# The mLSTM projection of a hybrid decoder as eight Strassen pairs, with y through DRAM

## The chip, the cores and the metric

The kernel runs on one core of a Trainium2 chip. The metric is the device time of one execution in microseconds (us); lower is better. Times of whole runs and the profiled execution are told apart below.

## What is computed

One layer of a decoder with two parallel branches, an mLSTM and a sliding-window attention with grouped queries, on 512 prompt tokens and 8 x 4 sample tokens: 544 columns of tokens in all, at a model width of 2048. The part that matters here is the merge:

```python
y = (jax.nn.sigmoid(g_m) * jnp.einsum('btc,cd->btd', br_m, w_proj_m)
     + jax.nn.sigmoid(g_a) * jnp.einsum('btc,cd->btd', br_a, w_proj_a))
out = jnp.einsum('btc,cd->btd', y, w_out)
return _layernorm(DN_ALPHA * x + out, ln_w, ln_b).astype(x.dtype)
```

`br_m` is the mLSTM branch's gated output and `br_a` the attention's; both are 2048 wide, as are the three weight matrices. Everything is float32.

## The kernel before

**Precision.** TensorE multiplies in its `fp32r` form. To keep float32's precision, each operand is split into a high part and the remainder: ScalarE (ACT) casts the high part, VectorE (DVE) subtracts it (`hilo`, lines 237 to 239, for operands; `split`, lines 194 to 200, for weights). A product is three matmuls: high by high, operand's remainder by weights' high part, operand's high part by weights' remainder.

**Layout.** Activations lie with their features on the 128 partitions: 16 tiles of 128 features, each with 544 token columns. A projection gives its output in 16 blocks `ct` of 128 features.

**The plain projection** (`gemm`, line 217, with `products`, line 202): for one block, two loads of 128 x 1024 weights (512 KB each), their splits, and for each of 16 tiles `k` of the contraction three products in two halves of 272 columns: 96 matmuls. The weights come through the pools `wr` (three raw buffers) and `wp` (two buffers of split weights), the result lies in one of two double banks of PSUM.

**The paired projection** (`paired`, line 643, with `prepare`, `half_product` and `gather`): for the input projection, two blocks of output are computed together by Strassen's scheme in Winograd's form. The contraction is cut in two halves of 8 tiles, the tokens in two halves of 272 columns (`HT`), and the two blocks are the third cut. Seven products of 8 x 3 = 24 matmuls, 168 in all, take the place of 192. The seven operands (`XS`) are quarters of the activations and sums of these; the sums of weights are made while the pairs run, some of them by DMAs of GpSimd that add (`acc`). A pair's two outputs lie in two of the three buffers of the pool `ev` until their `end` has stored them. The order of TensorE's instructions is the program's in this stage (`manual_schedule`); all other instructions are ordered ahead of time by the framework, which goes by the program's order, by priorities and by times that it simulates. Tiles of a pool get its buffers in the program's order.

**The stages around the change**, in order:

1. The 72 pairs of the input projection, with attention and the sample tokens' mLSTM in between. They store the sigmoids of the gates to DRAM (`d_sga`, `d_sgm`).
2. The attention's projection, lines 1415 to 1427: 16 plain blocks. A generator for the prompt's mLSTM is stepped every two `k` (`every=2`), and stores `d_brm`. Each block is multiplied by its gate and stored to `d_t`. When the mLSTM is done, its pools are closed (`esA`), and `branch` (line 1227) begins to load `d_brm` and split it, 16 loads of 272 KB and 16 splits, as the operand of the next stage, in a pool `act3` of eight tiles.
3. The mLSTM branch's projection, lines 1429 to 1438: 16 plain blocks. Each block loads its gate and its `d_t`, multiplies and adds, and splits the result at once into `yh` and `yl`, which stay in SBUF in the pool `act` as the next operand.
4. The output projection, lines 1571 to 1605: 13 plain blocks, three more in another form, and the residual and layer norm. Its pool `d1` (z, lw, lb: the input rows, the norm's weights and biases; z is loaded in four pieces of 1 MB, lw and lb are 1 MB each) is opened when the pools of stage 3 are closed.

SP (SyncE) issues all loads and stores here, one after the other; GpSimd issues the adding DMAs.

Of the kernel before, what the change touches and what calls it, by code (L numbers as in the profile page):

```python
# [15 lines left out]
F32 = mybir.dt.float32  # L16
F32R = mybir.dt.float32r
AF = mybir.ActivationFunctionType
ALU = mybir.AluOpType
# [4 lines left out]
NTS = 4  # L24
NS = NB * NTS
T = SEQ + NS
KT = D // 128
MH = 4
MD = 512
# [50 lines left out]
def _build(tc, nc, i, o, es):  # L80
# [11 lines left out]
    V, A, G, PE = nc.vector, nc.scalar, nc.gpsimd, nc.tensor  # L92

    cst = pool(es, "cst", 1, side="left")
    act = pool(es, "act", 8, side="left")
    wr = pool(es, "wr", 3)
    wp = pool(es, "wp", 2)
    evp = pool(es, "ev", 3)
# [19 lines left out]

    def ev(n=T):
        return evp.tile([128, n], F32, tag="ev", name=nm("ev"))  # L120
# [4 lines left out]
    def two(ap):  # L125
        return ap.rearrange("p (a b) -> p a b", a=2)
# [7 lines left out]
    def spawn(g):  # L134
        live.append(g)
# [81 lines left out]
    def gemm(wv, c0, xh, xl, cols=EVEN, raws=(None, None), every=8, prio=0, before=None):  # L217
        ps = mm()
        for half in range(2):
            if before:  # L220
                before(half)
            raw = raws[half] or load_half(wv, c0, half)
            if prio:
                with tc.high_priority(offset=prio):
                    wh, wl = split(raw)
            else:
                wh, wl = split(raw)
            products(ps, half, wh, wl, xh, xl, cols, every)
        return ps

    def pv(ps, r=ALL):
        return ps[r, :, :272]
# [8 lines left out]
    def act_tiles(p, s):  # L241
        return [p.tile([128, 4, T], F32R, tag="act", name=nm(s)) for _ in range(4)]
# [2 lines left out]
        return lambda k, c, w: tiles[k // 4][:, k % 4, c:c + w]  # L245

    HT = T // 2  # L250

    def quad(p, s):
        return [p.tile([128, 8, HT], F32R, tag="act", name=nm(s + n)) for n in "hl"]
# [389 lines left out]
    def paired(work, first=iter(())):  # L643

        steps = [(w, n) for w in work for n in range(7)]
        ready = 0
        load_a(work[0])
        load_b(work[0])
        for at, (w, n) in enumerate(steps):

            while ready < min(at + 3, len(steps)):
                with tc.high_priority(offset=AHEAD):
                    prepare(*steps[ready])
                ready += 1
# [12 lines left out]
            tick()  # L667
# [559 lines left out]
    def branch(src, p, tmp, ahead=()):  # L1227

        hs, los = act_tiles(p, "bh"), act_tiles(p, "bl")

        def steps():
            for k in range(KT):
                if k < len(ahead):
                    st = ahead[k]
                else:
                    st = tmp(k)
                    nc.sync.dma_start(st[:], src[k])
# [176 lines left out]
    bmh = None  # L1414
    for ct in range(16):
        sg = c5t()
        nc.sync.dma_start(sg[:], d_sga[ct])
        ps = gemm(wa_, ct * 128, bah, bal, every=2)
        V.tensor_tensor(out=two(sg[:]), in0=pv(ps), in1=two(sg[:]), op=ALU.mult)
        nc.sync.dma_start(d_t[ct], sg[:])  # L1420
        if bmh is None and (not live or ct == 15):
            drain()
            esA.close()
            esE = ExitStack()
            act3 = pool(esE, "act3", 8)
            bmh, bml, g_ = branch(d_brm, act3, lambda k: c5t() if k % 2 else ev())
            spawn(g_)
    drain()
    yh_, yl_ = act_tiles(act, "yh"), act_tiles(act, "yl")
    yh, yl = whole(yh_), whole(yl_)  # L1430
    for ct in range(16):
        sg, tt = c5t(), ev()
        nc.sync.dma_start(sg[:], d_sgm[ct])
        nc.sync.dma_start(tt[:], d_t[ct])
        ps = gemm(wm, ct * 128, bmh, bml)
        V.tensor_tensor(out=two(sg[:]), in0=pv(ps), in1=two(sg[:]), op=ALU.mult)
# [167 lines left out]
    finish(1, LAST)  # L1604
    drain()
    esD.close()


# [26 lines left out]
```

## Time and profile before

| what | value |
|---|---|
| three runs, us | 2542.88, 2548.21, 2549.33; median 2548.21 |
| profiled execution | 2543.75 us, its span 2541.9 us, granted TensorE clock 0.994 |
| attention's projection | first matmul of its first block at 1806.68 us of the span |
| mLSTM branch's projection | to 2321.70, where the output projection's first matmul starts |
| DMA moved | 421.89 MB, 166 GB/s over the span |

How to read the rows that follow. In a row by window, the numbers are the window, then for each engine its busy time and the number of its instructions, then the granted share of TensorE's clock, the share of time in which the 16 DMA engines are busy, and GB/s. In a row of a timeline there are the start, the duration, the engine (SPq is SP's queue, which issues DMAs), the line, the operation, what it writes and reads, how many, and in brackets the idle time before it and what ended that. In a row of the chain there are the start, the duration, and what ran. In a row of groups there are the line, the engine and the operation, then busy time and the mean of one in ns, then idle time before it and what ended it. Matmuls overlap, so what one costs in a stream is the distance of their starts, not its own duration.

### The profile page before, as it was taken

How to read it: one execution, taken by the hardware profiler on the slowest of the kernel's cores; microseconds unless marked ns; L12 is line 12 of the kernel's file. 1: busy time of each engine (PE TensorE's matmuls, PEld its weight loads, DVE VectorE, ACT ScalarE, POOL GpSimd, SP SyncE). 2: the span in 40 equal slices, each digit the busy share in tenths (PEclk: the TensorE clock that was granted, in tenths of full speed). 3: DMA queues.
4: the chain of work that ended last, by engine and by line, in shares of the span. 5: the costliest groups of instructions: out<-in, count | busy, mean ns of one | idle time of the engine just before them, and what ended most of it. 6: DMA issues, size and time to landing. Idle time of an engine off the chain costs nothing.

```text
span 2541.9 us, 48994 instructions
## 1 busy us (share of the span) xinstructions
PE 2509.8 (99%) x19995; PEld 2443.5 (96%) x19995; DVE 1709.8 (67%) x2506; ACT 1195.5 (47%) x1945; POOL 377.4 (15%) x434
## 2 busy tenths in 40 slices
PE   8999999999999999999999999999999999999997
PEld 7999999999999999999999999999999999999997
DVE  7867677777777777678787788777765653333236
ACT  4447667667667665443434544544533332222221
POOL 2111121111211211132022133121000000000002
PEclk9999999999999999999999999999999999999999
DMA  6566666666666654477577477477654555446332
GB/s 193 136 166 154 161 148 159 153 150 163 147 157 156 151 149 117 108 213 244 154 225 236 137 234 223 139 234 232 216 177 163 168 175 158 132 132 192 109 94 86
DMA packets 537105, 421.89 MB, mean 166 GB/s; under 512 B 43536, under 2 KB 449344, under 8 KB 536592
## 3 DMA queue, kind: packets, MB, share of 16 engines
q1 hardware_dynamic: 526800, 382.05, 50.8%
q0 software_dynamic: 10080, 36.70, 7.9%
q8 instruction: 157, 2.57, 0.4%
q14 instruction: 68, 0.56, 0.1%
HBM read 297.67 MB, written 86.42 MB: 151 GB/s over the span
## 4 chain that ended last, share of the span: by engine, by line
PE 57%; DVE 1%; issue 0%; POOL 0%; DVEq 0%
PE mm L207 21%; PE bank L610 18%; PE bank L612 9%; PE sm L1298 2%; PE sm L1101 1%; PE sm L1330 1%; PE sm L1343 1%; PE sm L207 1%; PE sm L1114 1%; DVE z L1537 0%; PE sm L1277 0%; PE sm L1285 0%; PE sm L1353 0%; DVE z L1542 0%; PE sm L1480 0%
## 5 line engine op out<-in xcount | busy, mean ns | idle before, releaser
L198 ACT CAST wh<-raw 128x1024 fp32r<-128x1024 f32 x604 | 632.3, 1048 | 918.9 <-PE bank L610 505.5
L199 DVE TENSOR_TENSOR wl<-raw,wh 128x1024 fp32r<-128x1024 f32 x604 | 756.5, 1254 | 360.5 <-ACT wh L198 353.1
L610 PE MATMUL bank<-xk,wh 128*128 128x272 f32 x2304 | 318.3, 291 | 0.0
L610 PEld LDWEIGHTS bank<-xk,wh 128*128 128x128 f32 x2304 | 299.5, 189 | 10.0 <-ACT wh L198 7.5
L590 DVE TENSOR_TENSOR raw<-raw,raw 128x1024 f32<-128x1024 f32 x218 | 278.4, 1278 | 6.3 <-DMA raw<-in_w_in 3.4
L207 PE MATMUL mm<-bh,wl 128*128 128x272 f32 x1024 | 214.4, 289 | 0.0
L207 PE MATMUL mm<-bh,wh 128*128 128x272 f32 x1024 | 214.2, 290 | 0.0
L207 PE MATMUL mm<-bl,wh 128*128 128x272 f32 x1024 | 213.4, 288 | 0.0
L612 PE MATMUL bank<-xk,wl 128*128 128x272 f32 x1152 | 167.5, 288 | 0.0
L629 POOL TENSOR_TENSOR ev<-p,ev 128x272 f32<-128x272 f32 x72 | 102.3, 1421 | 428.8 <-ACT ev L628 410.7
L207 PEld LDWEIGHTS mm<-bh,wh 128*128 128x128 f32 x1024 | 160.5, 188 | 2.3 <-issue 2.3
L207 PEld LDWEIGHTS mm<-bl,wh 128*128 128x128 f32 x1024 | 161.8, 188 | 0.0
L207 PEld LDWEIGHTS mm<-bh,wl 128*128 128x128 f32 x1024 | 160.6, 188 | 0.0
L612 PEld LDWEIGHTS bank<-xk,wl 128*128 128x128 f32 x1152 | 154.1, 189 | 0.0
L610 PE MATMUL bank<-n2h,wh 128*128 128x272 f32 x576 | 148.9, 291 | 2.0 <-ACT wh L198 2.0
L610 PE MATMUL bank<-a11h,wh 128*128 128x272 f32 x576 | 149.3, 291 | 0.0
L610 PE MATMUL bank<-s1h,wh 128*128 128x272 f32 x576 | 149.1, 292 | 0.1
L610 PE MATMUL bank<-s4h,wh 128*128 128x272 f32 x576 | 149.0, 292 | 0.0
L610 PE MATMUL bank<-n3h,wh 128*128 128x272 f32 x576 | 148.1, 290 | 0.0
L610 PE MATMUL bank<-a11l,wh 128*128 128x272 f32 x576 | 147.9, 289 | 0.0
L610 PE MATMUL bank<-n2l,wh 128*128 128x272 f32 x576 | 147.3, 288 | 0.0
L610 PE MATMUL bank<-n3l,wh 128*128 128x272 f32 x576 | 146.8, 287 | 0.0
(435 smaller groups left out, 5475.4 us busy)
## 6 DMA issues: line engine op xcount, KB each, us to landing
raw<-in_w_in SPq DMA_DIRECT2D x296, 512.0 KB
raw<-raw POOLq DMA_DIRECT2D x70, 512.0 KB, 4.9
C<-in_state_mlstm_C SPq DMA_DIRECT2D x32, 1024.0 KB
out<-C SPq DMA_DIRECT2D x64, 512.0 KB
raw<-in_w_proj_a SPq DMA_DIRECT2D x32, 512.0 KB
raw<-in_w_proj_m SPq DMA_DIRECT2D x32, 512.0 KB
raw<-in_w_out SPq DMA_DIRECT2D x32, 512.0 KB
d_sgm<-ev SPq DMA_DIRECT2D x16, 272.0 KB
```

The lines of the kernel that those rows point to most:

```text
L198: A.copy(wh[:], raw[:])
L199: V.tensor_tensor(out=wl[:], in0=raw[:], in1=r32(wh[:]), op=ALU.subtract)
L207: PE.matmul(ps[:, f, :w], a[:, kk], b(k, c, w), start=(k == 0 and n == 0), stop=(k == 15 and n == 2))
L590: V.tensor_tensor(out=w[out][:], in0=w[a][:], in1=w[b][:], op=ALU.add)
L610: PE.matmul(ps, wh[:, k], x(p, k), start=(first and k == 0 and p == 0), stop=False, skip_group_check=True)
L612: PE.matmul(ps, wl[:, k], x(0, k), start=False, stop=(k == 7), skip_group_check=True)
L629: G.tensor_tensor(out=c22, in0=p1, in1=c11, op=ALU.subtract)
L1101: PE.matmul(pC[b * 32:b * 32 + 32, :], qz[:, b], ct[:, b], start=True, stop=True, tile_position=(0, b * 32))
L1114: PE.matmul(pus[b][:], Ab[rows, c * 128:c * 128 + 128], r["V4"][rows], start=True, stop=True, tile_position=(b * 32, 0))
L1298: PE.matmul(pp[:, 0:258], a[:, b * 128:b * 128 + 128], b_[:, b, f], start=(b == 0 and n == 0), stop=(b == 3 and n == 2))
L1330: PE.matmul(pp[:, 0:n], x_[c][:, b * 128:b * 128 + 128], y_[c][:, b * 128:SEQ], start=(c == 0 and m == 0), stop=(c == 3 and m == 2))
L1343: PE.matmul(pp[:, 0:258], x_[:, off:off + 128], y_[:, b, f], start=(b == 0 and n == 0), stop=(b == j and n == 2))
```

## The change

The mLSTM branch's projection becomes eight pairs, run by the `paired` of the input projection with adding DMAs.

- Seven operands are needed. Four (`f11`, `f1`, `f2`, `f12`) are built by `first_forms` while the rest of the attention's projection runs, at the place where `branch` stood, in `act3`; two of the sums on the way are stored to DRAM (`d_n3`, `d_s4`). Three (`f3`, `f4`, `f22`) are loaded and split by `last_forms` while the first pair's first products run, in `act`, which the attention's operand leaves. A pool `fr` of four buffers serves these loads.
- Each pair loads its two gates and two tiles of `d_t` into `fr` at its fifth product (`fetch`, called in `paired`), multiplies and adds at its end, and stores y to DRAM (`d_y`). The last pair's two tiles of y stay in SBUF.
- After the pairs, 14 tiles of y are loaded from `d_y` through `ev`, and all 16 are split into `yh` and `yl`, which now lie in `act3`, in the buffers that the first four forms leave. Then `act` and the pairs' pools are closed, and the output projection follows as before, `d1` in the memory that they leave.

```diff
@@ pools and DRAM
-    act = pool(es, "act", 8, side="left")
+    esL = es.enter_context(ExitStack())
+    act = pool(esL, "act", 8, side="left")
...
+    d_y = dr.tile([16, 128, T], F32, name="d_y")
+    d_n3 = dr.tile([8, 128, HT], F32, name="d_n3")
+    d_s4 = dr.tile([8, 128, HT], F32, name="d_s4")
@@ paired
+            if n == 4 and "fetch" in w:
+                w["fetch"]()
@@ behind the mLSTM
+    def branch_part(k, c):
+        st = late["fr"].tile([128, 2, HT], F32, tag="fr", name=nm("fr"))
+        nc.sync.dma_start(st[:], d_brm[k:k + 2, :, c:c + HT].rearrange("k p t -> p k t"))
+        return st[:]
+
+    def first_forms(f11, f1, f2, f12):
+        for k in range(0, 8, 2):
+            ks = slice(k, k + 2)
+            r11, r21, r12, r22 = (branch_part(k_, c) for k_, c in ((k, 0), (k, HT), (k + 8, 0), (k + 8, HT)))
+            hilo(r11, f11[0][:, ks], f11[1][:, ks])
+            yield
+            hilo(r12, f12[0][:, ks], f12[1][:, ks])
+            V.tensor_tensor(out=r22, in0=r22, in1=r21, op=ALU.subtract)
+            yield
+            hilo(r22, f1[0][:, ks], f1[1][:, ks])
+            V.scalar_tensor_tensor(r21, r11, -1.0, r21, op0=ALU.mult, op1=ALU.subtract)
+            nc.sync.dma_start(d_n3[ks].rearrange("k p t -> p k t"), r21)
+            yield
+            V.tensor_tensor(out=r11, in0=r11, in1=r22, op=ALU.subtract)
+            hilo(r11, f2[0][:, ks], f2[1][:, ks])
+            yield
+            V.tensor_tensor(out=r12, in0=r12, in1=r11, op=ALU.subtract)
+            nc.sync.dma_start(d_s4[ks].rearrange("k p t -> p k t"), r12)
+            yield
+
+    def last_forms(f3, f4, f22):
+        for dst, src in ((f3, d_n3), (f4, d_s4), (f22, d_brm[8:16, :, HT:T])):
+            for k in range(0, 8, 2):
+                ks = slice(k, k + 2)
+                st = late["fr"].tile([128, 2, HT], F32, tag="fr", name=nm("fr"))
+                nc.sync.dma_start(st[:], src[ks].rearrange("k p t -> p k t"))
+                with tc.high_priority(offset=AHEAD):
+                    hilo(st[:], dst[0][:, ks], dst[1][:, ks])
+            yield
+
+    def merged(p):
+        w = dict(wv=wm, cA=p * 256, cB=p * 256 + 128, scale=1.0, acc=True)
+        def fetch():
+            w["in"] = []
+            for d_ in (d_sgm, d_t):
+                for ct in (2 * p, 2 * p + 1):
+                    st = late["fr"].tile([128, T], F32, tag="fr", name=nm("fr"))
+                    nc.sync.dma_start(st[:], d_[ct])
+                    w["in"].append(st)
+        def end(o1, o2):
+            g1, g2, t1_, t2_ = w["in"]
+            for ct, o, g, t_ in ((2 * p, o1, g1, t1_), (2 * p + 1, o2, g2, t2_)):
+                V.tensor_tensor(out=g[:], in0=o[:], in1=g[:], op=ALU.mult)
+                V.tensor_tensor(out=g[:], in0=g[:], in1=t_[:], op=ALU.add)
+                if p < 7:
+                    nc.sync.dma_start(d_y[ct], g[:])
+                else:
+                    late[ct] = g
+        w.update(fetch=fetch, end=end)
+        return w
@@ in the attention's projection, when the mLSTM is done
-            act3 = pool(esE, "act3", 8)
-            bmh, bml, g_ = branch(d_brm, act3, lambda k: c5t() if k % 2 else ev())
-            spawn(g_)
+            act3 = pool(esE, "act3", 8)
+            late["fr"] = pool(esR, "fr", 4)
+            wr2 = pool(esR, "wr2b", 3)
+            pe_ = pool(esR, "peb", 1)
+            f11, f1, f2, f12 = (quad(act3, n_) for n_ in ("f11", "f1", "f2", "f12"))
+            spawn(first_forms(f11, f1, f2, f12))
@@ the projection itself
-    yh_, yl_ = act_tiles(act, "yh"), act_tiles(act, "yl")
+    f3, f4, f22 = (quad(act, n_) for n_ in ("f3", "f4", "f22"))
+    XS = [quarter(f) for f in (f11, f1, f2, f12, f3, f4, f22)]
+    with tc.manual_schedule(engines={PE.engine}):
+        open_psum(True)
+        paired([merged(p) for p in range(8)], last_forms(f3, f4, f22))
+    open_psum(False)
+    yh_, yl_ = [], []
+    for q in range(4):
+        for tiles, n_ in ((yh_, "yh"), (yl_, "yl")):
+            tiles.append(act3.tile([128, 4, T], F32R, tag="act", name=nm(n_)))
     yh, yl = whole(yh_), whole(yl_)
     for ct in range(16):
-        sg, tt = c5t(), ev()
-        nc.sync.dma_start(sg[:], d_sgm[ct])
-        nc.sync.dma_start(tt[:], d_t[ct])
-        ps = gemm(wm, ct * 128, bmh, bml)
-        V.tensor_tensor(out=two(sg[:]), in0=pv(ps), in1=two(sg[:]), op=ALU.mult)
-        V.tensor_tensor(out=sg[:], in0=sg[:], in1=tt[:], op=ALU.add)
-        hilo(sg[:], yh_[ct // 4][:, ct % 4], yl_[ct // 4][:, ct % 4])
-    esE.close()
-    esC.close()
+        st = late.get(ct)
+        if st is None:
+            st = ev()
+            nc.sync.dma_start(st[:], d_y[ct])
+        hilo(st[:], yh_[ct // 4][:, ct % 4], yl_[ct // 4][:, ct % 4])
+    esR.close()
+    esL.close()
```

`esE` and `esC` are closed at the end of the kernel instead.

More of the change, by code (lines that the diff above doesn't have):

```diff
@@ L26 @@
 T = SEQ + NS
+HT = T // 2
 KT = D // 128
@@ L245, in whole @@
         return lambda k, c, w: tiles[k // 4][:, k % 4, c:c + w]
-    HT = T // 2
     def quad(p, s):
@@ L1413, in _build @@
     spawn(mlstm())
-    bmh = None
+    esE, esR, late = ExitStack(), ExitStack(), {}
+    def branch_part(k, c):
[21 more added lines that the diff above has]
+            yield
@@ L1420, in _build @@
         nc.sync.dma_start(d_t[ct], sg[:])
-        if bmh is None and (not live or ct == 15):
+        if "fr" not in late and (not live or ct == 15):
             drain()
             esA.close()
-            esE = ExitStack()
             act3 = pool(esE, "act3", 8)
-            bmh, bml, g_ = branch(d_brm, act3, lambda k: c5t() if k % 2 else ev())
-            spawn(g_)
-    drain()
-    yh_, yl_ = act_tiles(act, "yh"), act_tiles(act, "yl")
+            late["fr"] = pool(esR, "fr", 4)
[3 more added lines that the diff above has]
+            spawn(first_forms(f11, f1, f2, f12))
+    drain()
+    f3, f4, f22 = (quad(act, n_) for n_ in ("f3", "f4", "f22"))
[8 more added lines that the diff above has]
+            tiles.append(act3.tile([128, 4, T], F32R, tag="act", name=nm(n_)))
     yh, yl = whole(yh_), whole(yl_)
     for ct in range(16):
-        sg, tt = c5t(), ev()
-        nc.sync.dma_start(sg[:], d_sgm[ct])
-        nc.sync.dma_start(tt[:], d_t[ct])
-        ps = gemm(wm, ct * 128, bmh, bml)
-        V.tensor_tensor(out=two(sg[:]), in0=pv(ps), in1=two(sg[:]), op=ALU.mult)
-        V.tensor_tensor(out=sg[:], in0=sg[:], in1=tt[:], op=ALU.add)
-        hilo(sg[:], yh_[ct // 4][:, ct % 4], yl_[ct // 4][:, ct % 4])
-    esE.close()
-    esC.close()
+        st = late.get(ct)
[5 more added lines that the diff above has]
+    esL.close()
     esD = ExitStack()
@@ L1606, in _build @@
     esD.close()
+    esE.close()
+    esC.close()
 _INS = ["x_prompt", "x_sample", "state_mlstm_C", "state_mlstm_n", "state_mlstm_m", "state_attn_k", "state_attn_v",
```

## The prediction

> **What bounds the kernel now.** I read the page first, then the chain of work that ended last over the projections, then busy time by window, then the timelines of single engines at the two seams that the change makes.
>
> ```profile
> PE 2509.8 (99%) x19995; PEld 2443.5 (96%) x19995; DVE 1709.8 (67%) x2506; ACT 1195.5 (47%) x1945; POOL 377.4 (15%) x434
> ...
> 2099.93 240.00 PE mm L207 x1915
> ...
> 138.00:180.00 42.00, 42.00 (x338) 42.00 (x337) 26.52 (x29) 20.04 (x26) 6.74 (x7) 1.00 0.76 182
> 2060.00:2130.00 70.00, 70.00 (x560) 69.97 (x559) 28.63 (x35) 22.43 (x28) 0.00 (x0) 1.00 0.66 213
> 2130.00:2320.00 190.00, 190.00 (x1519) 190.00 (x1518) 69.36 (x78) 42.52 (x47) 0.00 (x0) 1.00 0.44 130
> ```
>
> TensorE is the bound: in 2130:2320, the mLSTM projection, it has no idle time, while VectorE is busy 69.36 of 190 us and the DMA engines 0.44. The chain is one piece of 1915 matmuls in 240.00 us, 0.1253 us each, across both projections and into the output projection. So every matmul taken out of this stage is worth 0.1253 us, as long as nothing else becomes late.
>
> **The matmuls removed.** Before, 16 blocks of 96 matmuls: 1536 x 0.1253 = 192.5 us. After, 8 pairs of 7 products of 24 matmuls: 1344. A pair bare of other work is in the trace: the window 138:180 holds two pairs, 338 matmuls by the count (2 x 168 and two cut by the window's edges) in 42.00 us, with no idle time. That is 21.0 us each, and 8 x 21.0 = 168.0 us. Term: **-24.5 us**. The counts are fixed by the loops, so the change cannot fail to do this much.
>
> **The pairs' other work.** Each pair's end adds four VectorE operations, and its loads and stores pass DRAM.
>
> ```profile
> L1436 DVE TENSOR_TENSOR c<-mm,c 128x544 f32<-128x544 f32 x15 | 10.9, 725 | 58.8 <-PE mm L207 58.8
> ...
> 89.00:110.00 21.00, 21.00 (x170) 21.00 (x169) 19.75 (x36) 8.87 (x13) 3.04 (x5) 1.00 0.59 145
> 1650.00:1782.00 132.00, 132.00 (x1031) 121.33 (x1030) 104.61 (x120) 58.97 (x76) 26.80 (x39) 1.00 0.75 237
> ```
>
> VectorE: 26.52 / 2 = 13.3 us a pair now, plus 4 x 0.725 = 2.9, so 16.2 of 21; the first pair (89:110) ran at 19.75 of 21.00 and TensorE lost nothing. DMA: that stage already stores two 272 KB tiles a pair; four loads come on top, 1.1 MB in 21 us, 53 GB/s on 182, so 235. The window 1650:1782 moved 237 GB/s with TensorE at 132.00 of 132. SP issues four more loads a pair; the weight loads stand in the same queue behind them, and these have most of a pair's 21 us. GpSimd issues the two adding DMAs a pair as in earlier pairs. Pair 0 also splits f3, f4 and f22: 12 x 0.72 (a split of that size, DVE L239 in the third fence) = 8.6 us of VectorE, which makes about 22 us in the 21 us of that pair with some of it done in the last block before; the cover is the room until products 4, 5 and 6 need them, 12 to 18 us in. If that cover went, it would be a stall of 2 to 3 us once. I take **+1** for the eight pairs (0 to 5).
>
> **The forms built behind the attention's projection.** They replace the old operand's 16 loads and splits by the same number of loads and splits, 16 more VectorE operations (11.6 us) and 8 stores of 272 KB. In 2060:2130 VectorE is busy 28.63 of 70 us, so this fits. Its four steps hang on each other by four buffers: loads, splits and the store behind them make about 12 us a step (two transfers of 4.3 us and some five operations of 0.7, by the rows of the next fence), 50 us from where the old operand was loaded (2072 there) to about 2122. The projection ends at 2321.7 - 192.5 = 2129. Cost 0; the cover is these 7 us, and beyond them each us is a us of waiting ahead of the first pair.
>
> **The seam behind the pairs: y comes back from DRAM.** Before, each block's y is split while the next block runs, and the output projection begins with no gap (row below, 2321.70). After, y of 14 of 16 blocks is loaded again through `ev`, a pool of three buffers, which the pairs use for their two outputs. What a buffer's round costs is in the attention's projection, where the operand is loaded the same way:
>
> ```profile
> 2321.70 0.41 PE L207 MATMUL mm<-yh,wh 128*128 128x256 f32 x2
> ...
> 2072.20 0.76 SPq L1237 DMA_DIRECT2D c<-d_brm  x1
> 2077.96 0.37 SPq L1237 DMA_DIRECT2D c<-d_brm  x1
> ...
> 2076.48 0.65 ACT L238 CAST bh<-c 128x544 fp32r<-128x544 f32 x1 [0.44 <-DMA c<-d_brm]
> ...
> 2077.21 0.72 DVE L239 TENSOR_TENSOR bl<-c,bh 128x544 fp32r<-128x544 f32 x1
> ...
> 1784.02 0.32 SPq L1172 DMA_DIRECT2D d_sga<-ev  x1
> 1787.87 0.32 SPq L1237 DMA_DIRECT2D ev<-d_bra  x1
> ...
> 1809.73 1.70 SPq L1237 DMA_DIRECT2D ev<-d_bra  x2
> ```
>
> Issue at 2072.20, cast begins at 2076.48 (the cast waited for it), split done at 2077.93, next load into that buffer at 2077.96. So 4.28 us to land, 5.8 us a round. The rows of 1784 to 1809 show the same seam once: behind the last pair of the earlier stage one load gets a buffer early (1787.87), the next two only after that pair is over (1809.73), because its two outputs hold the others.
>
> Call E the end of the last pair. The pair before it frees a buffer some 3 us into the last pair, and its first operand's memory, which takes the first y, is free after one product, so from E-18 one buffer works alone: y0 at -18, y1 -12.2, y2 -6.5, y3 -0.7. The last pair's outputs come free when they have been multiplied: some 0.7 us for its last subtraction (an operation of half the size, and its start), 0.725 each for multiply, add, multiply: y4 at 1.5, y5 at 2.9. What happens next decides the case. The memory for z, lw and lb is the one that the pairs' pools and `act` hold, so those loads start when the two y that stay on chip are split: last add done at 3.6, then 0.65 and 0.72 for cast and split, E+5.1 with the gaps. In the kernel before they start at the same sign:
>
> ```profile
> 2324.44 0.72 DVE L239 TENSOR_TENSOR yl<-c,yh 128x544 fp32r<-128x544 f32 x1
> ...
> 2325.02 0.52 SPq L1458 DMA_DIRECT2D z<-in_x_prompt  x1
> ...
> 2336.12 0.38 SPq L191 DMA_DIRECT2D raw<-in_w_out  x1
> 2336.55 5.59 SPq L1466 DMA_DIRECT2D lb<-in_ln_b  x1
> ...
> 2347.32 1.05 ACT L198 CAST wh<-raw 128x1024 fp32r<-128x1024 f32 x1 [6.55 <-DMA raw<-in_w_out]
> ...
> 2325.00:2350.00 25.00, 25.00 (x202) 24.99 (x202) 5.84 (x7) 5.35 (x8) 0.00 (x0) 1.00 1.00 324
> ```
>
> That burst fills all DMA engines for 25 us (share 1.00, 324 GB/s), and a weight load issued within it landed after 11.2 us (2336.12 to 2347.32). Before, nobody needed data then. After, ten loads of y stand in it. By these rows: y6 to y8 are issued at 5.1, 7.3 and 8.7, a round of 11.2 + 1.5 = 12.7, ready at 17.8, 20.0 and 21.4. The third round lies between 5.8 and 12.7 (the burst ebbs); I take 9, nearer to the middle: 26.8, 29.0, 30.4. The last round is quiet: y12 at 32.6, y13 at 34.8. The block's last three steps of six matmuls take 2.25: its end is E+37.0.
>
> TensorE isn't idle all that time, if the order of its queue lets the second block go ahead where the first lacks an operand. At the earlier seam it did:
>
> ```profile
> 1806.60:1829.00 22.40, 18.41 (x137) 17.57 (x137) 1.00 0.63 198
> ...
> 1829.10 0.72 DVE L1419 TENSOR_TENSOR c<-mm,c 128x544 f32<-128x544 f32 x1 [0.27 <-PE mm L207]
> ```
>
> 137 projection matmuls ran before the first block, which has 96, was complete (VectorE takes its result at 1829.10): some 41 are the second block's. Here the second block can go ahead by its first half alone, 48 matmuls, since the two pairs of weight buffers are taken. So 144 matmuls, 18.0 us, are done by E+37.0. Term: **+19.0 us** (y13 ready between 30 and 39: 14 to 23).
>
> **The clock.** The waits come in gaps of one to several us, and a gap costs more than itself:
>
> ```profile
> 118.58 0.39 PE L610 MATMUL bank<-n2h,wh 128*128 128x272 f32 x1 [1.97 <-ACT wh L198]
> ...
> 120.00:124.00 4.00, 4.00 (x24) 4.00 (x23) 1.45 (x2) 1.30 (x3) 0.86 (x1) 0.61 0.69 162
> ```
>
> After an idle time of 1.97 us the granted clock was 0.61 over 120:124, a loss of 0.39 x 4 = 1.6 us. Here most of a slower clock lies within the waiting; what counts is the end of the first block and the return to speed: **+2** (0 to 5). The Trainium skill (TensorE: Matmul & The Clock Gate, Part 1) has the clock halve only after an idle window of about 3.4 us, by which a 2 us gap would be free. The row disagrees; by that rule this term would be 0 as far as the gaps are short.
>
> **The sum** against the profiled execution (2543.75, its span 2541.9): -24.5 + 1 + 0 + 19.0 + 2 = -2.5, so 2541.3. The three runs have a median of 2548.21, 4.5 above the profiled one; on that footing 2545.7, rounded **2546**. About 0.3% (7.6 us) is what a measurement of this kernel tells from no change.
>
> **Rivals.**
> (a) *The burst misses the loads of y* (z's loads put behind them in SP's queue, or later). Every round 5.8: y13 issued at 1.5 + 3 x 5.8 = 18.9, ready 24.7, block done 26.9 to 28.4 with the second block's half; lost about 10, clock 2, pairs 1: -11.5, 2537. For: loads of y come first in the program. Against: at 2325 all of z went out at once as soon as its memory was free. 0.33. The Trainium skill (DMA: Bandwidth & Descriptors, Anatomy of one DMA) gives 2.0 us and the bytes over 436 GB/s for one transfer, 2.64 us for 272 KB as an estimate by that page, and by it this case would come to about 2529; the row says 4.28.
> (b) *Slower: TensorE keeps the blocks' order and stands until y13 is there.* The 48 matmuls don't go ahead (+6.0), and with the burst at full length through the third round (12.7 for 9) y13 is ready at 38.5: +3.7, clock +1: 2546 + 10.7 = 2556.7. It breaks even at y13 about E+31 and shows as slower from E+39. For: the order is fixed beforehand, by simulated landing times. Against: 137 matmuls above. 0.17.
>
> **How the numbers follow.** The forecast, burst and overtaking, has 0.50; its own range is 2539 to 2554. By its bounds it is within 0.3% with 0.80, faster 0.07, slower 0.13. (a) is faster with 0.85, else same; (b) slower with 0.62, else same. Faster 0.035 + 0.28 = 0.32; slower 0.065 + 0.105 = 0.17; same 0.51. The range takes (a) and (b) in: 2535 to 2557.
>
> **What would show it.** Right: eight pairs of 21.0 to 21.2 us from about 2129 to 2298; loads of `d_y` in threes; z's loads between the second and third three; TensorE waiting for `yh` or `yl` with some 20 us in all in the 40 us behind the pairs, the clock under 0.8 there; DMA share near 1. Wrong: pairs longer than 21.6 (VectorE or DMA bound after all); under 10 us of waiting (rival a); z's loads ahead of E or behind the last y; no waiting for y but one at the forms f3 to f22.

## The result, and the profile after

The changed kernel takes 2541.14 us (median of 20 executions, 2536.71 to 2550.3), the kernel before 2548.77 beside it (20 executions): ratio 0.9984, 95% interval 0.9976 to 0.9992. By the ratio that is 4 us or 0.16% faster, within the 0.3% that counts as no change. The two medians are 7.6 us (0.30%) apart, because the executions of one kernel scatter over 10 to 14 us and most of the changed kernel's lie low in their range, most of the other's high; this text goes by the ratio. The profiled execution took 2540.56 us with a span of 2538.8, 3.1 less than before. The forecast of 2541.3 for that execution and "same" held, and the median lies 5 us below its 2546. The sum did not come out as it was written, though: two of its terms were far off, in opposite directions.

The first rows of the page after, its engines; then busy time by window, over the seam ahead of the pairs (2129:2142), over pairs 1 to 7, and behind them:

```profile
PE 2488.7 (98%) x19803; PEld 2420.1 (95%) x19803; DVE 1785.6 (70%) x2606; ACT 1236.5 (49%) x2005; POOL 402.9 (16%) x458
```

```profile
2129.00:2142.00 13.00, 6.58 (x45) 6.38 (x45) 9.31 (x13) 4.82 (x7) 0.00 (x0) 0.82 0.97 244
...
2163.00:2310.00 147.00, 147.00 (x1175) 147.00 (x1175) 102.82 (x120) 59.38 (x72) 21.04 (x20) 1.00 0.89 228
2310.00:2316.00 6.00, 3.37 (x26) 2.96 (x24) 4.96 (x8) 2.89 (x4) 0.00 (x0) 1.00 0.67 204
2316.00:2330.00 14.00, 10.42 (x73) 9.32 (x74) 7.90 (x11) 6.37 (x10) 0.00 (x0) 1.00 0.74 230
```

TensorE has 192 matmuls less and 21.1 us less busy time. In pairs 1 to 7 it never stops: 1175 matmuls in 147.00 us, which is what was forecast. The time is lost on both sides of them: 6.58 busy of 13.00 ahead, 3.37 of 6.00 and 10.42 of 14.00 behind. The chain of waits, which was one piece of 1915 matmuls before, now has DMAs in it at both places:

```profile
2106.12 5.45 DMA fr<-d_brm
2116.84 3.74 DMA d_s<-fr
2120.60 5.87 DMA fr<-d_n
2127.71 2.63 DVE f3l L244 x4
2131.13 6.74 DMA fr<-d_s
2140.07 3.96 PE bank L612 x16
...
2306.90 3.41 DMA ev<-d_y
2314.52 4.20 DMA ev<-d_y
2320.16 2.52 DMA ev<-d_y
2324.14 2.68 DMA ev<-d_y
```

**Ahead of the pairs.** TensorE ends the attention's last block at 2133.65 and starts the first pair at 2140.07. Who it waited for, and the timeline of VectorE, ScalarE and SP's queue:

```profile
PE bank L612 <- DVE c L1484: 6.4, 1, 6.4
```

```profile
2136.25 3.05 DVE L244 TENSOR_TENSOR f4l<-fr,f4h 128x544 fp32r<-128x544 f32 x4 [3.51 <-ACT f4h L243]
2139.21 0.72 DVE L1484 TENSOR_TENSOR c<-mm,c 128x544 f32<-128x544 f32 x1
...
2135.57 0.64 ACT L243 CAST f4h<-fr 128x544 fp32r<-128x544 f32 x1 [7.49 <-DMA fr<-d_s]
...
2128.46 3.21 SPq L1452 DMA_DIRECT2D fr<-d_s  x4
```

Line 1484 multiplies the last block's result with its gate and so clears the PSUM bank. It had its operand at 2133.65 and started at 2139.21, because four splits of the form f4 stood ahead of it in VectorE's queue, and these waited for loads of `d_s4` that were issued from 2128.46, when the four buffers of `fr` came free, and landed in a window with a DMA share of 0.97. VectorE kept to the order that was fixed beforehand: it was idle for 3.51 us ahead of these splits, and for the last 2.6 of these us the block's multiplication, which stood behind them, was ready. The splits themselves then took another 3 us.

**Behind the pairs.** The last product of the last pair ends at E = 2310.55. SP's queue, then VectorE, then TensorE:

```profile
2306.90 0.32 SPq L1511 DMA_DIRECT2D ev<-d_y  x1
...
2309.83 2.26 SPq L1511 DMA_DIRECT2D ev<-d_y  x2
...
2314.52 9.94 SPq L1511 DMA_DIRECT2D ev<-d_y  x7
...
2326.73 0.96 SPq L1511 DMA_DIRECT2D ev<-d_y  x2
2327.73 0.42 SPq L1532 DMA_DIRECT2D z<-in_x_prompt  x1
```

```profile
2311.01 0.73 DVE L244 TENSOR_TENSOR yl<-ev,yh 128x544 fp32r<-128x544 f32 x1 [1.21 <-ACT yh L243]
2311.65 0.72 DVE L1472 TENSOR_TENSOR fr<-fr,fr 128x544 f32<-128x544 f32 x1
2312.29 0.43 DVE L641 SCALAR_TENSOR_TENSOR ev<-bank,p 128x272 f32<-128x272 f32 x1
...
2328.16 1.35 DVE L244 TENSOR_TENSOR yl<-fr,yh 128x544 fp32r<-128x544 f32 x2
```

```profile
PE mm L212 <- ACT yh L243: 2.9, 2, 2.0
PE mm L212 <- DVE ev L641: 2.3, 1, 2.3
PE mm L212 <- DVE yl L244: 0.8, 3, 0.3
```

z's first load is issued right behind the last load of y, at E+17.2. It did not wait for the two y that stay on chip: their splits (`yl<-fr`) start only at 2328.16, and the rest of z follows them from 2329.92. So its place in SP's queue, behind all loads of y, held it back. The burst missed y, and y13's split ended at 2333.35 = E+22.8. TensorE waited 6.2 us in all, 2.3 of them for the last gather (line 641), which again stood behind a split that waited.

### The profile page after: what moved, and what is told of

It reads as the page before. It is cut to its first block, busy times and chain, and to the rows that moved or that the text cites. A ratio compares the mean times of both kernels' runs of the same rounds, so it can differ in the third digit from the quotient of the medians.

```text
span 2538.8 us, 49027 instructions
## 1 busy us (share of the span) xinstructions
PE 2488.7 (98%) x19803; PEld 2420.1 (95%) x19803; DVE 1785.6 (70%) x2606; ACT 1236.5 (49%) x2005; POOL 402.9 (16%) x458
## 4 chain that ended last, share of the span: by engine, by line
PE 54%; DMA 2%; DVE 2%; issue 0%; ACT 0%; POOL 0%; SPq 0%; DVEq 0%; ACTq 0%
PE bank L612 22%; PE mm L212 11%; PE bank L614 11%; PE sm L1302 2%; PE sm L1105 1%; PE sm L1334 1%; PE sm L1347 1%; PE sm L212 1%; DMA raw<-in_w_out 1%; PE sm L1118 1%; DMA ev<-d_y 1%; DVE z L1611 0%; DMA z<-in_x_prompt 0%; PE sm L1281 0%; PE sm L1357 0%
## 5 line engine op out<-in xcount | busy, mean ns | idle before, releaser
L203 ACT CAST wh<-raw 128x1024 fp32r<-128x1024 f32 x628 | 657.3, 1048 | 827.9 <-PE bank L612 595.4
L204 DVE TENSOR_TENSOR wl<-raw,wh 128x1024 fp32r<-128x1024 f32 x628 | 785.6, 1253 | 297.2 <-ACT wh L203 292.8
L592 DVE TENSOR_TENSOR raw<-raw,raw 128x1024 f32<-128x1024 f32 x234 | 298.0, 1275 | 13.1 <-DMA raw<-in_w_proj_m 6.1
L631 POOL TENSOR_TENSOR ev<-p,ev 128x272 f32<-128x272 f32 x80 | 114.4, 1429 | 503.0 <-ACT ev L630 486.9
L590 POOL DMA_DIRECT2D raw<-raw x86 | 74.6, 868 | 458.0 <-DVE raw L592 173.7
L612 PE MATMUL bank<-s4l,wh 128*128 128x272 f32 x576 | 146.7, 287 | 0.0
L612 PE MATMUL bank<-s1l,wh 128*128 128x272 f32 x576 | 146.6, 287 | 0.0
L637 DVE SCALAR_TENSOR_TENSOR ev<-bank,ev 128x272 f32<-128x272 f32 x80 | 35.3, 441 | 120.6 <-PE bank L614 115.5
L612 PEld LDWEIGHTS bank<-n2h,wh 128*128 128x128 f32 x576 | 108.2, 188 | 7.7 <-ACT ev L630 3.4
L612 PEld LDWEIGHTS bank<-s1h,wh 128*128 128x128 f32 x576 | 108.2, 188 | 5.7 <-ACT p L622 2.5
```

The lines of the kernel that those rows point to most:

```text
L203: A.copy(wh[:], raw[:])
L204: V.tensor_tensor(out=wl[:], in0=raw[:], in1=r32(wh[:]), op=ALU.subtract)
L590: G.dma_start(out=w[out][:], in_=w[b][:], accum_op=ALU.add)
L592: V.tensor_tensor(out=w[out][:], in0=w[a][:], in1=w[b][:], op=ALU.add)
L612: PE.matmul(ps, wh[:, k], x(p, k), start=(first and k == 0 and p == 0), stop=False, skip_group_check=True)
L631: G.tensor_tensor(out=c22, in0=p1, in1=c11, op=ALU.subtract)
```

## The experiments

In the single profiles of the changed kernel and the experiments, the attention's last block ended anywhere from 2129.2 to 2139.9 us. Most of that spread comes from stages ahead of the change: the attention's projection began at 1803.5 to 1814.9, and from its first product to its last it took 324.9 to 327.1 us (322.8 before the change). So the experiments are read by the two stretches that the change touches, and by the ratio to the kernel before, run beside each (its median lay between 2543.95 and 2548.77 us). "Head" is from the end of the attention's last block to the start of pair 1; undisturbed it would be 20.9 us (in e8, below). "Seam" is from the last pair's end to the last matmul on y; before the change these matmuls took 206.1.

| kernel | head, us | seam, us | ratio to before, 95% interval |
|---|---|---|---|
| before | | 206.1 | 1 |
| changed | 29.4 | 213.6 | 0.9984 (0.9976 to 0.9992) |
| e1_bank | 26.7 | 214.4 | 0.9966 (0.9953 to 0.9979) |
| e2_forms_behind | 22.0 | 213.5 | 0.9947 (0.9928 to 0.9966) |
| e3_forms_and_sum_behind | 22.1 | 216.5 | 0.9961 (0.9945 to 0.9978) |
| e4_kept_y_first | 28.3 | 236.1 | 1.0047 (1.0027 to 1.0066) |
| e5_five_buffers | 29.6 | 212.4 | 0.9969 (0.9957 to 0.9981) |
| e6_no_overtaking | 29.8 | 215.1 | 0.9978 (0.9968 to 0.9989) |
| e7_no_y_loads | 29.5 | 211.4 | 0.9984 (0.9971 to 0.9997) |
| e8_forms_behind_five_bank | 20.9 | 210.7 | 0.9933 (0.9915 to 0.9951) |
| e9_block_order | 30.1 | 220.0 | 1.0023 (1.0013 to 1.0032) |
| e10_two_y_loads | 30.0 | 205.9 | 0.9960 (0.9945 to 0.9975) |
| e11_splits_behind_gather | 29.7 | 213.5 | 0.9992 (0.9981 to 1.0002) |
| e12_five_edits | 20.9 | 213.0 | 0.9956 (0.9941 to 0.9971) |

How far the stretches scatter can be read from kernels whose edits leave them alone: the head is 28.3 to 30.1 us in the changed kernel, e4 to e7 and e9 to e11, the seam 213.5 to 216.5 in the changed kernel, e2, e3 and e6. Each is one profile, so smaller differences show nothing by themselves.

The theory after the result was: the head is lost to VectorE's queue (f4's splits ahead of the last block's result), the seam to y's loads, one buffer after the other, with z's burst out of the way. Rivals: the head is lost to the change of PSUM pools (the pairs' banks open only when all of the block's banks are clear); the seam is lost to something else than y.

**e1, the banks.** The PSUM pools wait for the single tile whose memory they take, not for the whole pool:

```diff
         if space is None:
             kw["side"] = side or "right"
+        if space in (None, PSUM):
             kw["reuse_waits"] = "tile"
```

> The PSUM pools give back single banks instead of waiting for the whole pool, so the first pair's first product needs no bank of the last attention block. Queue theory (VectorE stands in its queue at f4's splits, which wait for a load, and everything behind them is late): the 6.4 us in front of the first product goes, but the second product then waits for its weights, whose split stands behind the same f4 splits; the first seven products together end at most 3 us sooner, time 0 to 3 us below the changed kernel. Bank theory (the wait is the swap of the PSUM pools): the 6.4 us go and nothing takes their place, 6 to 8 us below.

TensorE's waits in the stretch:

```profile
PE bank L613 <- DVE c L1485: 3.4, 1, 3.4
PE bank L613 <- ACT wh L204: 0.2, 1, 0.2
```

The first product no longer waits, but a later one of the same pair does, for the same operation (now line 1485): the head is 2.8 us shorter of 8.5 lost. The time by the ratios is lower too, but the intervals of the two kernels overlap. The bank decides where the wait is met and a third of its price, not that it is there.

**e2, the forms behind.** The splits of f4 and f22 are tied behind the split of the third weights on ScalarE and VectorE:

```diff
+    if dst is f3:
+        behind = state["wh"].ins, state["wl"].ins
-    with tc.high_priority(offset=AHEAD):
+    with tc.high_priority(offset=AHEAD), ExitStack() as q_:
+        if dst is not f3:
+            [q_.enter_context(tc.issue_after(b_)) for b_ in behind]
         hilo(st[:], dst[0][:, ks], dst[1][:, ks])
```

> The splits of f4 and f22 are ordered behind the splits of the first pair's third weights on VectorE and ScalarE; banks as in the changed kernel. Queue theory: the last attention block's multiplication runs at once, the first pair starts within 1.5 us of the block's end instead of 6.4 and takes 21 to 22 us instead of 23: 6 to 9 us below the changed kernel. Bank theory: the wait in front of the first pair stays above 5 us and the time is within 1 us of the changed kernel.

VectorE, and TensorE's waits in the stretch:

```profile
2132.27 0.72 DVE L1488 TENSOR_TENSOR c<-mm,c 128x544 f32<-128x544 f32 x1 [0.96 <-PE mm L212]
...
2137.69 2.63 DVE L244 TENSOR_TENSOR f4l<-fr,f4h 128x544 fp32r<-128x544 f32 x4
```

```profile
PE bank L612 <- ACT wh L203: 0.9, 1, 0.9
```

The block's result (now line 1488) is taken as soon as TensorE delivers it, f4 follows 5.4 us later and nobody waits for it: the head is 7.4 us shorter, the time 0.37% lower by the ratios, and the intervals of the two kernels are apart. So the queue was the cause, and the cover for the forms was real, only unused.

**e3, the sum as well.** In the last block and the one before it TensorE also lost 1.97 and 0.84 us, its weights' splits standing behind the sum of the first pair's weights and behind a form's subtraction, which waited for loads. Here the sum (line 592) is tied behind the first pair's first split, on top of e2:

```diff
         if n == 1:
             w["t1"] = raw2()
-            add("t1", "b11", "b12")
+            with tc.issue_after(state["wl"].ins) if "fetch" in w else ExitStack():
+                add("t1", "b11", "b12")
```

> As the run before, and the first sum of two raw weights of the first pair is ordered behind the split of its first weights, so that the last attention block's second weights don't wait behind it. Queue theory: the gap of 1.97 us in the last attention block goes too, with 1 to 2 us of clock: 8 to 12 us below the changed kernel. Rival (these gaps cover each other: what is not lost in the block is lost in front of the first pair): the same time as the run before within 1 us.

The gap at the sum went, but the one before it grew from 0.84 to 1.87 us, a weights' split behind a subtraction that had waited 3.38 us for its load:

```profile
2118.39 0.73 DVE L1434 TENSOR_TENSOR fr<-fr,fr 128x544 f32<-128x544 f32 x1 [3.38 <-DMA fr<-d_brm]
2119.03 1.22 DVE L204 TENSOR_TENSOR wl<-raw,wh 128x1024 fp32r<-128x1024 f32 x1
```

No gain over e2 is shown, and the intervals overlap: a miss. The head is the same; the seam is 3 us longer than in e2 behind a wait of 5.4 us for the last gather (2.3 in e2), which the edit doesn't touch.

**e4, the burst.** The two y that stay on chip are split first in the program, so that z's loads come early, as the forecast had assumed:

```diff
-    for ct in range(16):
+    for ct in (14, 15, *range(14)):
         st = late.get(ct)
```

> The two tiles of y that stay on chip are split first, so the buffers under z, lw and lb come free early and their 6 MB of loads start among the loads of y, as the forecast had it. Burst theory of the forecast: loads of y issued within it land after 8 to 12 us instead of 4 to 5, and what is lost behind the pairs is 17 to 23 us instead of 8: 9 to 15 us above the changed kernel. Rival (loads of 272 KB pass between the large ones): at most 3 us above.

SP's queue, the cast of the y that the marked load brings, and TensorE's waits:

```profile
2317.37 0.38 SPq L1532 DMA_DIRECT2D z<-in_x_prompt  x1
...
2330.31 0.38 SPq L1511 DMA_DIRECT2D ev<-d_y  x1
...
2342.70 0.65 ACT L243 CAST yh<-ev 128x544 fp32r<-128x544 f32 x1 [12.17 <-DMA ev<-d_y]
```

```profile
PE mm L212 <- ACT yh L243: 19.8, 5, 11.3
```

z is loaded from E+2.7, a load of y issued at 2330.31 is cast 12.4 us later, and the seam is 22.5 us longer than in the changed kernel. The forecast's mechanism exists, at the forecast's price or more: the seam is 30.0 us above the 206.1 of before, where the forecast had 19.0 and 2 for the clock. By the ratios the kernel is 16 us slower than the changed one, just above the 9 to 15 expected; its executions lie between 2555 and 2568 us, and the profiled one is among the slow ones. Only the condition did not hold in the changed kernel.

**e5, five buffers for y.**

```diff
-            st = ev()
+            st = c5t() if ct % 2 else ev()
             nc.sync.dma_start(st[:], d_y[ct])
```

> Every other load of y takes one of two further buffers, so five instead of three loads of y can be under way. Theory that the seam's 8.2 us are y's loads waiting for buffers (issued one or two at a time from 2295.46 to 2326.73, the next one only when a split has freed a buffer): y13's split is done about 14 us after the last pair's last product instead of 22.9, the waits inside w_out's first two blocks of columns fall from 6.2 us to 2.3 to 3, and the kernel is 3 to 5 us below the changed one, 2536 to 2538. Rival, that the loads are held by the DMA share (0.74 in those 14 us) or that the casts and splits hold y: no more than 1 us below the changed kernel, with the loads issued earlier and landing as much later.

The last split of y ends 17.6 us after the last pair, not 22.8, and the waits for y are gone. Another takes their place:

```profile
PE mm L212 <- DVE ev L641: 3.9, 1, 3.9
PE mm L212 <- ACT wh L203: 0.9, 1, 0.9
```

The waits sum to 5.0 us where they were 6.2, and the seam is 1.2 us shorter. By time it lies below the changed kernel (2538.68; 0.9969 against 0.9984), but the intervals overlap slightly. Between theory and rival: the buffers were a limit for y, and of the 3.7 us of waiting for y that went, 2.5 came back at the gather, which now stood behind a weights' split that had waited 2.65 us for its cast, and at the first weights. The clock took some more: it was 0.50 in 2318.65:2321.15, where the changed kernel's seam had 1.00 throughout. A gain in time is not shown.

**e6, no overtaking.** The edit wraps `gemm` for w_out's first two blocks in a region where TensorE keeps the program's order:

```diff
-        ps = gemm(wo, ct * 128, yh, yl, cols=CUT, raws=raws)
+        with tc.manual_schedule(engines={PE.engine}) if ct < 2 else ExitStack():
+            ps = gemm(wo, ct * 128, yh, yl, cols=CUT, raws=raws)
```

> w_out's first two blocks of columns are put out in the program's order, so that TensorE cannot take the second block's products while the first one's next y is late. Theory that the overtaking hides y's lateness: each of the 48 products of the second block that ran early was cover, 48 x 0.1253 = 6.0 us, so the seam's waits rise from 6.2 to 11 to 13 us and the kernel is 5 to 7 us above the changed one, 2546 to 2548. Rival, that the sum of the waits is set elsewhere (y is early enough for the order not to matter): within 1 us of the changed kernel.

It did not bind: TensorE's instructions stood in the same order as in the changed kernel. So this run says nothing of overtaking and is only a second look at the changed kernel, of use for the clock (last section).

**e7, no loads of y.**

```diff
-            st = ev()
-            nc.sync.dma_start(st[:], d_y[ct])
+            st = late[14 + ct % 2]
```

> This kernel leaves out the 14 loads of y from DRAM: all 16 y tiles are splits of the last pair's two kept tiles (so w_out gets a wrong operand by design of the experiment); casts, splits and products stay. Theory that y's loads are what the seam waits for: the waits inside w_out's first two blocks fall from 6.2 us to 2 to 3 (the first, for the last gather, stays), the kernel is 3 to 5 us below the changed one, 2536 to 2538; this bounds what any way of loading y earlier can bring. Rival, that the casts on ScalarE and splits on VectorE of 16 tiles hold the seam: the waits stay above 5 us, within 1 us of the changed kernel.

Nothing of y is loaded here: all 16 tiles are split from the last pair's two. The waits fall from 6.2 to 4.4 us, but 3.7 of them are for the first cast: all y now hangs on the last pair's end. The time shows no gain. The run was badly built as a bound; e10 is the better one.

**e9, block order.** The second block's products are tied behind the first one's last:

```diff
+        with tc.issue_after(state["mm"].ins) if ct == 1 else ExitStack():
             ps = gemm(wo, ct * 128, yh, yl, cols=CUT, raws=raws)
```

> The sixth run's edit did not bind: its products stood in the same order as the changed kernel's. Here the second block's first product is tied behind the first block's last one. Theory that the overtaking covers y's lateness: in the changed kernel y13's split ended 22.9 us after the last pair, with 18 products of the first block behind it and the 96 of the second all but the 48 that overtook; in block order 48 x 0.1253 = 6.0 us of products stand behind y13 that stood ahead of it, less what little of the 192 was late for other reasons: the stretch from the last pair to the last product 4 to 6 us longer than the changed kernel's 213.6, the kernel at 2545 to 2547. Rival, that y's lateness is already spent in the waits of the first block (6.2 us) and the order does not matter: within 1 us.

```profile
PE mm L212 <- ACT yh L243: 5.2, 3, 2.4
PE mm L212 <- DVE ev L641: 2.5, 1, 2.5
PE mm L212 <- DVE yl L244: 0.8, 3, 0.3
```

The seam is 6.4 us longer, and the ratio rises by 0.39%, some 10 us, of which the two intervals leave 5 to 14. When the last split of y ended, 78 products of w_out had run, against 119 in the changed kernel: 41 fewer, or 5.1 us at 0.1253 each. So overtaking was worth nearly what the forecast gave it, 6.0 us, and the rival falls. The rest of the 6.4 is y, 0.5 us later behind the last pair, and clock: 0.50 was granted in 2326.90:2331.90, behind a wait of 1.96 us, and 0.86 in 2341.90:2346.90, behind the last split.

**e10, two loads of y.**

```diff
-            st = ev()
-            nc.sync.dma_start(st[:], d_y[ct])
+            st = late[ct] = late[ct - 2] if ct > 1 else c5t()
+            if ct < 2:
+                nc.sync.dma_start(st[:], d_y[ct])
```

> This kernel loads only the first two of the 14 y tiles, into two further buffers, and takes their contents for the other twelve too (12 loads of y and its true contents are left out); all casts, splits and products stay, and nearly all splits of y come ahead of the last gather. The seventh run could not bound the loads, since there all y hung on the last pair. Theory that y's loads, and the queues behind casts that wait for them, are the seam: of its waits of 6.2 us at most 1.5 stay, and the stretch from the last pair to the last product falls from 213.6 to 207.5 to 209.5 (before the change its products took 206.1): 4 to 6 us below the changed kernel. Rival, that the seam is held by something else than y (the first product's bank, the first weights of w_out, the granted clock): the stretch stays above 211.

```profile
PE mm L212 <- DVE ev L641: 0.6, 1, 0.6
PE bank L612 <- DVE ev L637: 0.4, 1, 0.4
```

The seam is 205.9 us, as short as the matmuls alone before the change. No wait for y is left, and that for the gather is down to 0.6. By the ratios the kernel is 6.1 us below the changed one, and the intervals are apart. z's loads start at E+2.1 here and cost nothing, as no load of y is left among them. So y's loads and the queues behind them are the whole 7.5 us of the seam, and nothing is left for the rival.

**e11, the splits behind the gather.**

```diff
+        with tc.issue_after(state["c21"].ins) if ct > 1 else ExitStack():
             hilo(st[:], yh_[ct // 4][:, ct % 4], yl_[ct // 4][:, ct % 4])
```

> The splits of y from the third tile on are put behind the last gather's operation on VectorE (in the changed kernel that operation started 2312.29, behind a split that had waited 1.21 us for its cast, and TensorE's first product of w_out waited 2.31 us for it). Queue theory, as at the head: the first wait falls to 1 us or less, the kernel 1 to 2 us below the changed one. Rival, that y is then as late at the next tile: the first wait falls and the waits of y grow by as much, no more than 0.5 us below.

The first wait fell from 2.3 to 0.6 us, and the waits for y came to 3.7 us, as in the changed kernel:

```profile
PE mm L212 <- ACT yh L243: 3.2, 3, 1.3
PE mm L212 <- DVE yl L244: 0.5, 2, 0.3
```

The seam is the same within 0.1 us, and no change of time is shown. So the result is the rival's, though the waits for y did not grow: TensorE ran slowly instead, at 0.54 in 2318.19:2325.69. y13's split ended 22.8 us behind the last pair in both kernels, with 118 products of w_out done here and 119 there. Whether the gain would have gone without the slow clock is not shown. Unlike the head, where the waiting work had slack, here the next thing late is y itself.

**e8 and e12, the edits together.** e8 has the edits of e1, e2 and e5, e12 that of e11 as well.

> Three edits together: the splits of the forms f4 and f22 put behind the last weights' split (as in the second run, 6 us below the changed kernel in time, 7.4 us in the stretch from the block's end to pair 1), five buffers for y's loads, and the PSUM pools that wait for the single tile they reuse (as in the first run, 2.8 us in that stretch, of which the first edit already holds most). If the head and the seam add: 6 to 7.4, plus 3 to 5, plus 0 to 1: 9 to 13 below the changed kernel, 2528 to 2532, faster than both kernels. If the seam's waits are not the buffers': 6 to 8 below the changed kernel, as the second run alone, 2533 to 2535.

> The eighth run's three edits (2528.78) and the splits of y behind the last gather. In the eighth run the first product of w_out waited 2.2 us, the last gather's operation standing behind a split and a sum on VectorE. If the queue is the cause there too: 1 to 1.5 us less than the eighth run, about 2527.5, and 18 us or more below the kernel before. If not: the eighth run's time again.

The head of e8 by window, all its time busy:

```profile
2129.15:2150.04 20.89, 20.89 (x169) 20.89 (x168) 17.70 (x22) 12.94 (x19) 3.43 (x3) 1.00 1.05 295
```

e8 takes 2528.78 us, ratio 0.9933 (0.9915 to 0.9951): 17 us faster than the kernel before, and 13 faster than the changed one by the ratios (8.5 from the head and 2.9 from the seam, by the stretches), as expected. e12 has the same head and nothing more from its further edit; it is not faster than e8.

## Why the prediction was right, and where it was wrong

Right in the total by luck: 13.5 us too much for the seam, 10.3 too little ahead of the pairs and 2.3 outside the sum nearly cancelled. Signs that the prediction itself had given for being wrong came true: TensorE waited 6.2 us behind the pairs and not some 20, and z's loads stood behind the last y. By its own steps, from the profiles:

| step | forecast, us | measured, us | from |
|---|---|---|---|
| matmuls removed | -24.5 | -24.2 | 8 x 21.04 instead of 192.5 |
| pairs' other work | +1 | +8.5 | head 29.4 less 20.9 |
| forms behind the attention's projection | 0 | +2.8 | gaps 0.84 and 1.97 |
| seam and clock | +21 | +7.5 | 213.6 less 206.1 |
| not in the sum | | +2.3 | the end of the attention's last block 1.6 later beyond those gaps (0.9 of it stood already at that projection's start), the tail 0.5, the rest rounding |
| sum | -2.5 | -3.1 | |

*Matmuls removed*: right, to 0.3 us.

*The pairs' other work* failed at "some of it done in the last block before; the cover is the room until products 4, 5 and 6 need them". The room was there; e2 used it. But the queue had f4's splits in the last block, ahead of that block's own result, and their loads were late. The price given for a lost cover, "a stall of 2 to 3 us once", counted the splits' own time and not what stands behind them while they wait for a DMA, nor the clock. Of the 8.5 us, 6.4 are the wait and 2.1 a clock of 0.58 over the 4.96 us that followed.

*The forms* failed at "so this fits. Cost 0". VectorE has the room that 28.63 of 70 us promised, and the forms were done by about 2117, ahead of the block's end. What cost was again the order: weights' splits behind sums that waited for loads. That these sums caused the gaps is read from the timeline; e3 moved one of them and showed no gain.

*The seam* failed at "those loads start when the two y that stay on chip are split ... E+5.1". They started at E+17.2, and the first of them ahead of these splits, in the changed kernel as in e4 (2317.37, where the splits begin at 2317.57). So readiness of the splits did not set it; the place in SP's queue did, which e4 shows to move with the place of the two splits in the program. With the burst out of the way the case was rival (a), whose rounds gave y13 ready at 24.7 (22.8 measured) and a loss of about 10 (7.5 measured); (a)'s own total was missed for the head's sake. e4 supplied the missing condition and got the burst's price. The seam was taken to hang on DMA, and e10 shows that it does.

*Overtaking*, 48 matmuls or 6.0 us, was nearly right: 41 by the end of y13's split, 5.1 us, and the seam is 6.4 longer without it (e9). Rival (b) had it wrong.

*The clock*, +2, fell in another place: 2.1 us in pair 0, and 1.00 throughout the seam. The latter was luck too, since in 11 of the 12 experiments some of the seam ran at half clock (last section). The Trainium skill (TensorE: Matmul & The Clock Gate, Part 1) lets gaps below about 3.4 us pass free; in the changed kernel's seam the trace agrees, with waits of 2.3 and 2.0 us at 1.00, in e6 (0.54 behind a wait of 1.98 us) and e9 (0.50 behind one of 1.96) it does not.

*Loads of y*: the four in the chain above took 2.5 to 4.2 us. The forecast's 4.28 is the upper end here. By the Trainium skill (DMA: Bandwidth & Descriptors, Anatomy of one DMA) 272 KB take 2.64 us as an estimate, for transfers that GpSimd issues; SP issues these, and the shorter two, 2.52 and 2.68, come out alike.

## What to carry to other kernels

An operation that is hidden by room on its engine can still cost its whole wait: look at what stands behind it in the engine's queue, and when its load lands, and not only at the engine's busy share. Where a stage is shortened, cost its two ends separately and by stretches, since errors of opposite sign can give a right total. Before freeing one wait, ask what is late next: at the head the delayed work had slack and 7.4 us came back, at the seam y13 came as late as before and nothing did.

## What the runs showed of the hardware that was not expected

The same waits need not give the same clock. In the changed kernel and in e6, which have the same order on TensorE, the waits behind the pairs were alike (2.31, 0.32 and 1.98 us; 2.21, 0.28 and 1.98), and the window 2320:2325 has 24 matmuls in both. The changed kernel's row, then that of e6:

```profile
2320.00:2325.00 5.00, 3.62 (x24) 3.18 (x25) 2.88 (x5) 3.01 (x6) 0.00 (x0) 1.00 0.51 167
```

```profile
2320.00:2325.00 5.00, 5.00 (x24) 4.88 (x23) 2.50 (x3) 2.97 (x5) 0.00 (x0) 0.54 0.71 211
```

In one the clock stayed at 1.00 and TensorE waited again, in the other it was 0.54 and no further wait shows. The seam differs by 1.5 us, so where operands come late anyway most of a slow clock is hidden in their lateness.

What decides it can be read from the kept traces. In each of them every slow stretch begins a whole multiple of 3.413 us from every other, and runs at 0.50 for 3.41 us or a multiple of it: the time of an execution is cut in windows of that length. Two of the changed kernel's windows behind the last pair, then two of e6:

```profile
2311.51:2314.93 3.42, 2.06 (x16) 2.09 (x17) 3.38 (x6) 1.14 (x3) 0.00 (x0) 1.00 0.78 261
2314.93:2318.34 3.41, 2.20 (x16) 1.76 (x14) 1.59 (x3) 0.57 (x1) 0.00 (x0) 1.00 0.95 281
```

```profile
2314.38:2317.79 3.41, 1.69 (x12) 1.30 (x10) 1.03 (x2) 0.41 (x2) 0.00 (x0) 1.00 1.03 330
2317.79:2321.20 3.41, 2.87 (x11) 2.61 (x12) 2.12 (x3) 1.78 (x3) 0.00 (x0) 0.50 0.45 142
```

In the changed kernel the waits are spread so that TensorE is busy for 2.06 us of a window or more; in e6 it is busy for 1.69 in one, and the next is slow. Taken over the changed kernel and all experiments between 2050 and 2500 us, of the windows at full clock, all 19 with TensorE busy for less than 44% were followed by half clock, 6 of the 16 with 44 to 60%, and none of the 72 partly idle ones with more. So a wait of about 2 us costs the clock or not by where it falls in these windows, and the windows lie differently in executions of nearly the same code. This is read from traces alone; no run moved a wait on purpose, and what decides between 44 and 60% stays open.
